# Order of the seven block products in the feed-forward down projection, and the order of token tiles in the last two

## The chip, the cores and the metric

The kernel runs on one core of one Trainium2 chip. The metric is the device time of one execution in microseconds (us). A core has a matrix engine (PE, with its own queue for weight loads, PEld), a vector engine (DVE), a scalar engine (ACT), a general engine (POOL), and a queue engine (SP) that only issues DMA transfers. Each takes its own list of instructions in order; semaphores tie them together. Matmul results go to PSUM, in banks of 128 partitions by 512 float32; everything else is in SBUF.

## The reference

A trunk of two encoder layers on 512 tokens of width 1024. Layer 0 mixes tokens by dilated window attention, layer 1 by latent attention; behind each mixer stands a squared-ReLU MLP of width 4096:

```python
def sq_relu_mlp(h, w1, w2):
    a = jax.nn.relu(h @ w1)
    return (a * a) @ w2

for i in range(DEPTH):
    h = rms_norm(x, norm_mix[i])
    x = x + (dilated_mixer(h, ...) if i % 2 == 0 else mla_mixer(h, ...))
    h = rms_norm(x, norm_ffn[i])
    x = x + sq_relu_mlp(h, ffn_w1[i], ffn_w2[i])
```

The change touches the second product of the MLP, `(a * a) @ w2`, in both layers.

## The kernel before

**Precision.** Every float32 operand of these matmuls is split into a rounded part and a rest: ACT copies the value to `hi` (type fp32r), DVE subtracts to get `lo`. A product of two such values is three matmuls: hi·hi, hi·lo, lo·hi. So each weight tile costs one ACT and one DVE instruction ahead of its matmuls. The split weights (`whi`, `wlo`) sit in four buffers each, in turn; a fifth split waits until the matmuls have let go of the first.

**The MLP** (`mlp`, L592). The width 4096 is cut into four pieces `ch` of 1024. `up(ch, grp)` (L597) makes half a piece: four 128-row groups of `a2`, each by 48 matmuls of 512 columns over four weight units (`run_block`, L161), then Relu and Square on ACT (L615, L616). `down(ch)` (L620) multiplies the piece by its 1024 rows of `w2` and adds it to `resid`. The order is up(0,0), up(0,1), then for each of three pieces up(ch+1,0), down(ch), up(ch+1,1), and at the end down(3). So the last piece stands directly behind up(3,1), which makes the second half of the very piece that it reads; the others have half an up block between.

**The down product** (`wino`, L489). The 512 x 1024 by 1024 x 1024 product is done as a 2 x 2 block product with seven block products in place of eight. `Aq(i, j)` is the block of token half i and inner half j: rows 4j to 4j+3 of `a2` (so `Aq(0, 0)` needs only what up(ch,0) made, and every `Aq(., 1)` needs up(ch,1) too). Three of the left operands are sums of blocks, made on DVE into the two tiles `S["c"]` and `S["d"]` (`stmp`, L514): product 5 uses c = Aq(1,0) - Aq(1,1); product 3 uses d = c - Aq(0,0) and then c = d + Aq(0,1); product 6 uses d; product 7 uses c = Aq(0,0) - Aq(1,0). Products 1, 2 and 4 read blocks of `a2` as they are. Each left operand is split by `split_a` (L483) into one of four `asp` buffers.

The right operands are blocks of `w2` or sums of them, built by DMA in four slots of `wqs`. A plain block is fetched on SP (L511). A sum is a plain fetch and then an accumulating DMA on POOL (L509) onto the same slot; slot `sT` serves 5, then has a block added for 6, then another for 4. The adding DMA has to wait until the earlier product's splits have read the slot. Slots change roles from piece to piece (L583 to L586): the next piece's `sT` is this piece's slot of product 3, its slot of product 1 is this piece's of product 7, of 3 this piece's of 1 (and 2), and of 7 this piece's `sT`.

**Chains and banks.** A product is 24 matmuls: two halves u of the inner dimension, two token tiles t, two 128-rows each, three matmuls. `ORDER` (L588) gives each product a chain of two PSUM banks. Chain a (pool `sc_p`) takes products 1, 6, 7 and 4, each added onto the sum before; chain b takes 5 and 3, chain d product 2, both in pool `tp_p`. After each product `put` (L551) adds the chain's two banks onto a block of `resid` on DVE, one instruction a token tile. A product that adds onto a chain can't write a bank before `put` of the product before it has read it.

**What follows the last piece.** `done` is called for each finished block of `resid`. In layer 1 it writes the block out (L912). In layer 0 (`done0`, L659) it starts the norm of a token tile once both column halves are complete (`norm_tile`, L206: square on ACT, power on POOL, scaling on DVE, then transposes on PE into `tp_p` banks and the split of the result by ACT and DVE into `hT`), and the latent projection of layer 1 (`b_w_in`, L862) follows, 24 matmuls of 448 columns for each of four token tiles.

**Order of execution.** The context at L941 asks for a planned schedule: each engine's list isn't the written order but one that a planner lays out under the written dependencies. In the trace the first half of product 2 runs ahead of product 7, though it is written behind it.

Of the kernel before, what the change touches and what calls it, by code (L numbers as in the profile page):

```python
# [13 lines left out]
ALU = mybir.AluOpType  # L14
# [73 lines left out]
def encoder_kernel(ctx: ExitStack, tc: tile.TileContext, x, norm_mix, norm_ffn, a_w_qkv, a_q_gain, a_k_gain,  # L88
# [6 lines left out]
    def nm(s):  # L95
        uid[0] += 1
        return f"{s}_{uid[0]}"
# [13 lines left out]
    acc_p = ctx.enter_context(tc.tile_pool(name="acc_p", bufs=4, space=PSUM))  # L111
    tp_p = ctx.enter_context(tc.tile_pool(name="tp_p", bufs=2, space=PSUM))
    sc_p = ctx.enter_context(tc.tile_pool(name="sc_p", bufs=2, space=PSUM))
# [369 lines left out]
    def split_a(x, pool):  # L483
        t = pool.tile([P, 4, 2, 256], F32R, tag="asp", name=nm("asp"), bufs=4)
        A.activation(t[:, :, 0], x, AF.Copy)  # L485
        V.tensor_tensor(t[:, :, 1], x, t[:, :, 0].bitcast(F32), op=ALU.subtract)
        return t

    def wino(tag, Aq, w, wqs, pool, resid, done=None):  # L489

        v = w.rearrange("(k p) c -> p k c", p=P)
        S = {}
        slots = SLOTS[tag % 4]  # L500

        def fetch(slot, key, add=False):

            ki, ni = key
            for u in range(2):
                t = wqs[:, 2 * slot + u]
                src = v[:, 4 * ki + 2 * u:4 * ki + 2 * u + 2, 512 * ni:512 * ni + 512]
                if add:
                    nc.gpsimd.dma_start(t, src, accum_op=ALU.add)  # L509
                else:  # L510
                    nc.sync.dma_start(t, src)  # L511
            return [wqs[:, 2 * slot + u] for u in range(2)]

        def stmp(name, x, y, op):  # L514
            if name not in S:
                S[name] = pool.tile([P, 4, 256], F32, tag="S", name=nm("S"), bufs=2)
            V.tensor_tensor(S[name], x, y, op=op)
            return S[name]

        def split_w(x):  # L520
            hi = wp.tile([P, 2, 512], F32R, tag="whi", name=nm("whi"))
            lo = wp.tile([P, 2, 512], F32R, tag="wlo", name=nm("wlo"))
            A.activation(hi, x, AF.Copy)  # L523
            V.tensor_tensor(lo, x, hi.bitcast(F32), op=ALU.subtract)  # L524
            return hi, lo

        sT, s1, s3, s7 = slots
        fetch(sT, (0, 0))
        bT = fetch(sT, (0, 1), add=True)
        b1 = fetch(s1, (0, 0))  # L530
        b3 = fetch(s3, (1, 1))
        fetch(s7, (0, 1))
        b7 = fetch(s7, (1, 1), add=True)

        def operands(p):
            if p == 5:
                return stmp("c", Aq(1, 0), Aq(1, 1), ALU.subtract), bT
            if p == 1:
                return Aq(0, 0), b1
            if p == 3:  # L540
                stmp("d", S["c"], Aq(0, 0), ALU.subtract)
                return stmp("c", S["d"], Aq(0, 1), ALU.add), b3
            if p == 6:
                return S["d"], fetch(sT, (1, 1), add=True)
            if p == 7:
                return stmp("c", Aq(0, 0), Aq(1, 0), ALU.subtract), b7
            if p == 2:
                return Aq(0, 1), fetch(s1, (1, 0))
            return Aq(1, 1), fetch(sT, (1, 0), add=True)

        def put(i, n, op, banks):  # L551
            for t in range(2):
                sl = resid[:, 2 * i + t, 512 * n:512 * n + 512]
                V.tensor_tensor(sl, sl, banks[t], op=op)
                if done is not None and p in (2, 4, 6, 7):
                    done(2 * i + t, n)

        banks = {}
        for p, chain, first, (i, n, op) in ORDER:
            a, wq = operands(p)  # L560
            at = split_a(a, pool)
            if first:
                pl, tg = (sc_p, "sc") if chain == "a" else (tp_p, "tp")
                banks[chain] = [pl.tile([P, 512], F32, tag=tg, name=nm(tg)) for _ in range(2)]
            bk = banks[chain]

            tail = done is not None and p == 4
            parts = {}
            for u, t in ((0, 0), (1, 0), (0, 1), (1, 1)) if tail else ((0, 0), (0, 1), (1, 0), (1, 1)):
                if u not in parts:  # L570
                    parts[u] = split_w(wq[u])
                hi, lo = parts[u]
                for j in range(2):
                    k = 2 * u + j
                    ah = at[:, k, 0, t * P:(t + 1) * P]
                    al = at[:, k, 1, t * P:(t + 1) * P]
                    for i_, (lt, rt) in enumerate(((ah, hi), (ah, lo), (al, hi))):
                        PE.matmul(bk[t], lhsT=lt, rhs=rt[:, j], start=(first and k == 0 and i_ == 0),  # L578
                                  stop=(k == 3 and i_ == 2), skip_group_check=True)
            put(i, n, op, bk)  # L580
# [3 lines left out]
    for _ in range(3):  # L584
        t_, p_, q_, r_ = SLOTS[-1]
        SLOTS.append((q_, r_, p_, t_))  # L586

    ORDER = [(5, "b", True, (1, 1, ALU.add)), (1, "a", True, (0, 0, ALU.add)), (3, "b", False, (0, 1, ALU.add)),  # L588
             (6, "a", False, (0, 1, ALU.subtract)), (7, "a", False, (1, 1, ALU.subtract)),
             (2, "d", True, (0, 0, ALU.add)), (4, "a", False, (1, 0, ALU.add))]  # L590

    def mlp(layer, w1, w2, hT_m, resid, pool, done):  # L592
        a2s = {}
# [26 lines left out]
        def down(ch):  # L620
            a2 = a2s.pop(ch)
            wino(layer * 4 + ch, lambda i, j: a2[:, 4 * j:4 * j + 4, 256 * i:256 * i + 256],
                 w2[1024 * ch:1024 * ch + 1024, :], wqs, pool, resid, done if ch == 3 else None)
# [48 lines left out]
    if True:  # L672
        with tc.tile_pool(name="bpool", bufs=1, reuse_waits="tile") as bp, \
# [203 lines left out]
            pend, tail, nxt, pT, pTs = [], [], None, None, None  # L877
            plan = {2: [(kv_chunk, 0)], 3: [(kv_chunk, 1), (kv_chunk, 2)], 4: [(kv_chunk, 3), (q_chunk, 0)],
                    5: [(q_chunk, 1)], 6: [(q_chunk, 2)], 7: [(q_chunk, 3)]}
            for s_ in range(HB * NT + lag):  # L880
                p, c = divmod(s_, 8)
# [4 lines left out]
                if s_ >= lag:  # L886
                    d, h2, r2, f = pend.pop(0)
# [7 lines left out]
                if p + 1 < HB // 2:  # L895
                    if c == 2:
                        nxt = new_pair(p + 1)
                    if s_ < NT - 1:
                        tail = tail + [q_chunk(cur, s_ + 1)]
                    fresh = [fn(nxt, r) for fn, r in plan.get(c, [])]  # L900
                    if c == 7:
                        tail, fresh = tail + fresh, []
                    for f in tail:
                        f()
                    tail = fresh
# [40 lines left out]
```

## Time and profile before

| | us |
|---|---|
| median of three runs | 1466.03 |
| lowest and highest run | 1465.76, 1466.09 |
| the profiled execution | 1465.81 |
| its span in the profile | 1463.5 |
| PE busy, of the span | 1416.1 |
| DVE busy | 888.2 |
| ACT busy | 727.0 |
| POOL busy | 197.3 |
| the down products of layer 0 (start of the first, end of the last matmul) | 637.39 to 905.77 |
| the down products of layer 1 (the same) | 1191.85 to 1459.47 |

The profiled execution is within 0.3 us of the median; the 2.3 us between its time and its span lie ahead of and behind what the profile covers. Nearly the whole span is PE at work, so what counts is the few places where PE stands idle or runs at a lower clock. "Idle before, releaser" in a row of the timeline is how long the engine had been idle ahead of that instruction and what let it go; "PEclk" is the clock granted to PE as a share of the full one.

### The profile page before, as it was taken

How to read it: one execution, taken by the hardware profiler on the slowest of the kernel's cores; microseconds unless marked ns; L12 is line 12 of the kernel's file. 1: busy time of each engine (PE TensorE's matmuls, PEld its weight loads, DVE VectorE, ACT ScalarE, POOL GpSimd, SP SyncE). 2: the span in 40 equal slices, each digit the busy share in tenths (PEclk: the TensorE clock that was granted, in tenths of full speed). 3: DMA queues.
4: the chain of work that ended last, by engine and by line, in shares of the span. 5: the costliest groups of instructions: out<-in, count | busy, mean ns of one | idle time of the engine just before them, and what ended most of it. 6: DMA issues, size and time to landing. Idle time of an engine off the chain costs nothing.

```text
span 1463.5 us, 19306 instructions
## 1 busy us (share of the span) xinstructions
PE 1416.1 (97%) x7116; PEld 1203.2 (82%) x7116; DVE 888.2 (61%) x1421; ACT 727.0 (50%) x1590; POOL 197.3 (13%) x197
## 2 busy tenths in 40 slices
PE   7999999999999999999999989999999999999988
PEld 6889889889988878888888877776778888888877
DVE  6765565656547654364664758588755265574746
ACT  5544455355335623553635445687633453645543
POOL 1120120111011101010110131232201010010100
PEclk9999999999999999999999999999999999999999
DMA  6315214312532335667494843201014758494843
GB/s 226 105 51 166 62 44 138 95 61 67 160 94 65 96 135 154 207 132 213 118 228 105 218 105 81 67 30 30 30 43 127 219 118 227 103 226 120 202 98 87
DMA packets 134813, 177.52 MB, mean 121 GB/s; under 512 B 8768, under 2 KB 73536, under 8 KB 134720
## 3 DMA queue, kind: packets, MB, share of 16 engines
q1 hardware_dynamic: 117312, 142.74, 30.9%
q0 software_dynamic: 17408, 33.56, 14.1%
q8 instruction: 56, 0.92, 0.3%
q14 instruction: 37, 0.30, 0.1%
HBM read 172.07 MB, written 4.19 MB: 120 GB/s over the span
## 4 chain that ended last, share of the span: by engine, by line
PE 91%; DVE 3%; ACT 3%; issue 2%; DMA 1%; POOL 0%; SPq 0%; DVEq 0%; ACTq 0%; POOLq 0%
PE acc L184 57%; PE sc L578 12%; PE tp L578 9%; PE tp L123 4%; PE acc L857 1%; PE acc L833 1%; PE sc L751 1%; PE sco L444 1%; PE sco L440 1%; PE sc L351 1%; DVE wlo L158 1%; PE sc L833 1%; PE sc L344 0%; PE tp L857 0%; PE sc L340 0%
## 5 line engine op out<-in xcount | busy, mean ns | idle before, releaser
L184 PE MATMUL acc<-whi,hT 128*128 128x512 f32 (+2 forms) x1600 | 487.6, 380 | 7.7 <-DVE t L311 2.6
L158 DVE TENSOR_TENSOR wlo<-raw,whi 128x1024 fp32r<-128x1024 f32 (+3 forms) x170 | 195.8, 1156 | 241.1 <-ACT whi L157 236.3
L184 PEld LDWEIGHTS acc<-whi,hT 128*128 128x128 f32 x1600 | 297.0, 190 | 49.6 <-issue 3.2
L184 PE MATMUL acc<-hT_f,whi 128*128 128x512 f32 (+1 forms) x1152 | 322.7, 366 | 1.7 <-DVE resid L639 1.2
L157 ACT ACTIVATE whi<-raw 128x1024 fp32r<-128x1024 f32 (+3 forms) x170 | 170.3, 1005 | 268.3 <-PE acc L184 170.8
L184 PE MATMUL acc<-wlo,hT 128*128 128x512 f32 (+2 forms) x800 | 300.6, 376 | 0.0
L184 PEld LDWEIGHTS acc<-hT_f,whi 128*128 128x128 f32 x1152 | 208.2, 189 | 37.4 <-DVE resid L639 1.6
L524 DVE TENSOR_TENSOR wlo<-wqs,whi 128x1024 fp32r<-128x1024 f32 x112 | 137.1, 1224 | 123.3 <-ACT whi L523 123.2
L184 PE MATMUL acc<-hT_f,wlo 128*128 128x512 f32 (+1 forms) x576 | 207.7, 365 | 0.0
L523 ACT ACTIVATE whi<-wqs 128x1024 fp32r<-128x1024 f32 x112 | 118.8, 1060 | 170.4 <-PE sc L578 60.9
L184 PEld LDWEIGHTS acc<-wlo,hT 128*128 128x128 f32 x800 | 151.8, 190 | 20.0 <-DVE wlo L158 0.5
L578 PE MATMUL sc<-whi,asp 128*128 128x512 f32 x512 | 164.7, 391 | 0.0
L509 POOL DMA_DIRECT2D wqs<-in_ffn_w_dram x64 | 78.2, 1347 | 541.9 <-DVE wlo L524 283.9
L578 PE MATMUL tp<-whi,asp 128*128 128x512 f32 x384 | 125.1, 394 | 8.9 <-ACT asp L485 8.9
L184 PEld LDWEIGHTS acc<-hT_f,wlo 128*128 128x128 f32 x576 | 108.5, 189 | 17.5
L131 POOL TENSOR_TENSOR qrs<-rs_v,nhalf 128x4 f32<-128x4 f32 x48 | 61.5, 1290 | 408.6 <-DVE rs_v L128 394.1
L578 PEld LDWEIGHTS sc<-whi,asp 128*128 128x128 f32 x512 | 96.7, 189 | 20.1
L578 PE MATMUL sc<-wlo,asp 128*128 128x512 f32 x256 | 100.5, 393 | 0.0
L578 PEld LDWEIGHTS tp<-whi,asp 128*128 128x128 f32 x384 | 73.2, 191 | 25.0 <-ACT asp L485 9.7
L578 PE MATMUL tp<-wlo,asp 128*128 128x512 f32 x192 | 75.9, 395 | 0.0
L136 ACT ACTIVATE junk<-acc 128x128 f32<-128x128 f32 x192 | 53.0, 276 | 18.9 <-PE acc L184 13.9
L578 PEld LDWEIGHTS sc<-wlo,asp 128*128 128x128 f32 x256 | 48.6, 190 | 10.3
(185 smaller groups left out, 1771.0 us busy)
## 6 DMA issues: line engine op xcount, KB each, us to landing
wqs<-in_ffn_w_dram SPq DMA_DIRECT2D x80, 512.0 KB, 4.9
raw<-in_ffn_w_dram SPq DMA_DIRECT2D x64, 512.0 KB, 4.1
wqs<-in_ffn_w_dram POOLq DMA_DIRECT2D x64, 512.0 KB, 7.4
raw<-in_a_w_qkv_dram SPq DMA_DIRECT2D x96, 256.0 KB, 3.3
raw<-in_a_w_qkv_dram SPq DMA_DIRECT2D x64, 192.0 KB, 2.7
raw<-in_a_w_o_dram SPq DMA_DIRECT2D x8, 512.0 KB, 3.9
raw<-in_b_w_o_dram SPq DMA_DIRECT2D x8, 512.0 KB, 3.7
xt<-in_x_dram SPq DMA_DIRECT2D x8, 256.0 KB, 5.7
```

The lines of the kernel that those rows point to most:

```text
L123: PE.transpose(o, i, ident)
L131: G.tensor_tensor(out, v[:, :n], nhalf[:, :n], op=ALU.pow)
L136: A.activation(junk, x, AF.Square, scale=1.0 / math.sqrt(dim), accum_out=out)
L157: A.activation(hi[:, :nk, :n], raw[:, :nk, :n], AF.Copy)
L158: V.tensor_tensor(lo[:, :nk, :n], raw[:, :nk, :n], hi[:, :nk, :n].bitcast(F32), op=ALU.subtract)
L184: PE.matmul(accs[o][:, oc], lhsT=lt, rhs=rt, start=(kt == 0 and p_i == 0 and hv == 0), stop=(kt == total - 1 and p_i == 2), skip_group_che ...
L351: PE.matmul(sc[:, r * P:(r + 1) * P], lhsT=qT[:, r * P:(r + 1) * P], rhs=kT[:, r * P:(r + 1) * P], start=True, stop=True)
L509: nc.gpsimd.dma_start(t, src, accum_op=ALU.add)
L523: A.activation(hi, x, AF.Copy)
L524: V.tensor_tensor(lo, x, hi.bitcast(F32), op=ALU.subtract)
L578: PE.matmul(bk[t], lhsT=lt, rhs=rt[:, j], start=(first and k == 0 and i_ == 0), stop=(k == 3 and i_ == 2), skip_group_check=True)
L833: PE.matmul(sc, lhsT=lt, rhs=rt, start=(i == 0), stop=(i == 4))
```

## The change

Three things are edited. The products run in the order 1, 5, 3, 6, 2, 7, 4 in all eight pieces in place of 5, 1, 3, 6, 7, 2, 4, and slot `s1` is fetched ahead of `sT`. In the last piece of each layer (`done` given) the banks of chain d come from the four of `acc_p`, not from `tp_p`. And in those two pieces product 7, like product 4 before, does all of token tile 0 and then all of token tile 1.

```diff
         sT, s1, s3, s7 = slots
+        b1 = fetch(s1, (0, 0))
         fetch(sT, (0, 0))
         bT = fetch(sT, (0, 1), add=True)
-        b1 = fetch(s1, (0, 0))
         b3 = fetch(s3, (1, 1))
...
             if first:
-                pl, tg = (sc_p, "sc") if chain == "a" else (tp_p, "tp")
+                pl, tg = {"a": (sc_p, "sc"), "b": (tp_p, "tp"), "d": (tp_p, "tp")}[chain]
+                if done is not None and chain == "d":
+                    pl, tg = acc_p, "acc"
                 banks[chain] = [pl.tile([P, 512], F32, tag=tg, name=nm(tg)) for _ in range(2)]
...
-            tail = done is not None and p == 4
+            tail = done is not None and p in (7, 4)
...
-    ORDER = [(5, "b", True, (1, 1, ALU.add)), (1, "a", True, (0, 0, ALU.add)), (3, "b", False, (0, 1, ALU.add)),
-             (6, "a", False, (0, 1, ALU.subtract)), (7, "a", False, (1, 1, ALU.subtract)),
-             (2, "d", True, (0, 0, ALU.add)), (4, "a", False, (1, 0, ALU.add))]
+    ORDER = [(1, "a", True, (0, 0, ALU.add)), (5, "b", True, (1, 1, ALU.add)), (3, "b", False, (0, 1, ALU.add)),
+             (6, "a", False, (0, 1, ALU.subtract)), (2, "d", True, (0, 0, ALU.add)),
+             (7, "a", False, (1, 1, ALU.subtract)), (4, "a", False, (1, 0, ALU.add))]
```

## Prediction

> **What bounds the kernel.** The page first.
>
> ```profile
> PE 1416.1 (97%) x7116; PEld 1203.2 (82%) x7116; DVE 888.2 (61%) x1421; ACT 727.0 (50%) x1590; POOL 197.3 (13%) x197
> PE 91%; DVE 3%; ACT 3%; issue 2%; DMA 1%; POOL 0%; SPq 0%; DVEq 0%; ACTq 0%; POOLq 0%
> ```
>
> PE is busy 97% of the span and 91% of the chain that ended last, and the change takes no matmul away. So it can only win where PE idles or runs at a low clock. The waits of PE, by line, say where:
>
> ```profile
> PE tp L578 <- ACT asp L485: 8.9, 2, 4.4
> PE acc L184 <- ACT hT L220: 1.9, 2, 1.4
> PE tp L123 <- DVE hT L221: 1.9, 1, 1.9
> ```
>
> The down products (L578) wait twice, 4.4 us each. No `put` is in the list. Now an undisturbed piece in the chain of waits:
>
> ```profile
> 637.55 5.44 PE tp L578 x24
> 659.31 2.72 PE tp L578 x12
> 662.03 5.44 PE sc L578 x24
> 667.47 2.72 PE tp L578 x12
> ```
>
> 24 matmuls take 5.44 us, one 0.227, seven products 38.1. Half of product 2 (tp, x12) runs ahead of 7 (sc, x24): the planner had filled the place where 7 waits for the `put` of 6. The six inner pieces have no idle PE, so nothing is to be won there.
>
> The timeline at the start of layer 1's last piece:
>
> ```profile
> 1409.42 1.06 ACT L523 ACTIVATE whi<-wqs 128x1024 fp32r<-128x1024 f32 x1 [4.38 <-PE acc L184]
> 1414.66 0.39 PE L184 MATMUL acc<-hT_f,wlo 128*128 128x512 f32 x1
> 1414.89 1.04 ACT L523 ACTIVATE whi<-wqs 128x1024 fp32r<-128x1024 f32 x1
> 1416.45 0.63 ACT L616 ACTIVATE a<-a 128x512 f32<-128x512 f32 x1
> 1417.11 1.23 DVE L517 TENSOR_TENSOR S<-a 128x1024 f32<-128x1024 f32 x1
> 1418.37 1.06 ACT L485 ACTIVATE asp<-S 128x1024 fp32r<-128x1024 f32 x1 [1.29 <-DVE S L517]
> 1419.33 1.04 ACT L485 ACTIVATE asp<-a 128x1024 fp32r<-128x1024 f32 x1
> 1419.48 0.75 PE L578 MATMUL tp<-whi,asp 128*128 128x512 f32 x1 [4.43 <-ACT asp L485]
> 1419.51 1.22 DVE L486 TENSOR_TENSOR asp<-S,asp 128x1024 fp32r<-128x1024 f32 x1
> ```
>
> The last up matmul ends at 1415.05; its Square ends at 1417.08; then c for product 5 on DVE, its split on ACT, and PE starts 4.43 us late. Product 1's split (asp<-a) stands behind all that though it reads only the first half of `a2`. The clock then falls:
>
> ```profile
> 1419.40:1422.90 3.50, 3.42 (x8) 2.75 (x9) 3.50 (x4) 0.98 (x2) 0.00 (x0) 0.52 0.24 92
> 1423.00:1459.40 36.40, 36.40 (x161) 29.84 (x159) 26.66 (x30) 15.36 (x15) 2.44 (x2) 1.00 0.31 80
> 865.00:870.40 5.40, 5.38 (x13) 4.24 (x14) 4.46 (x4) 1.82 (x2) 5.40 (x6) 0.54 0.15 59
> 1459.51 0.69 DVE L554 TENSOR_TENSOR resid<-resid,sc 128x512 f32<-128x512 f32 x1 [2.03 <-PE sc L578]
> ```
>
> In these windows (length, then busy time and count of PE, PEld, DVE, ACT, POOL, then clock) 8 matmuls take 3.42 us in place of 1.81 in layer 1 and 13 take 5.38 in place of 2.95 in layer 0: 1.6 and 2.4 us lost to a clock of 0.52 to 0.54.
>
> **Part 1: product 1 first.** Counted whole, layer 1's last piece runs from 1415.05 to its last `put` at 1459.51, so PE needs 44.4 for 38.1 us of matmuls: 6.3 us too many. Layer 0's has the same 4.43 and 2.4 for the clock, 6.8. Together **13.1 us**. With 1 first, its left operand depends on up(3,0) alone. Its weights are split in time: the four `whi` buffers let three units of a piece be split before the last up matmul (the third at 1409.42) and the fourth at 1414.89. So 1 starts as the up block ends, and covers 5.44 us, to 1420.49. Product 5 needs its hi part by then (there at 1418.37 + 1.06 = 1419.43 now) and its lo part by its third matmul, at 1420.94 (now 1419.51 + 1.22 = 1420.73). It fits by 0.2 us. But 3's first weight unit comes free half a product on, at 1417.77, and its ACT copy (1.04) may go in front and delay both by 0.5, and in layer 0 POOL works beside these DVE steps:
>
> ```profile
> 862.65 1.22 DVE L517 TENSOR_TENSOR S<-a 128x1024 f32<-128x1024 f32 x1
> 865.19 1.48 DVE L486 TENSOR_TENSOR asp<-S,asp 128x1024 fp32r<-128x1024 f32 x1
> 865.55 1.44 POOL L689 TENSOR_TENSOR cgB<-ck,gr 128x128 f32<-128x128 f32 x1
> ```
>
> There the step takes 0.26 longer. Behind it DVE owes c and d for 3, its lo part, two `put`s and two weight rests by product 3's start, some 7 steps of 1.22 in the 8.8 us from 1417.11 to 1425.93: a stall of 0 to 1.5. I take 0.8 a piece: 13.1 - 1.6 = 11.5: **-11.5 us**.
>
> [...]
>
> **Part 2: the neighbours on one chain.** Before, 6 and 7 stood together on chain a. Now 5 and 3 do (chain b), and 7 and 4 (chain a).
>
> ```profile
> 642.54 1.28 DVE L554 TENSOR_TENSOR resid<-resid,tp 128x512 f32<-128x512 f32 x2
> ```
>
> Product 5 ends at 642.99 by the chain; its first `put` (half of 1.28) ends at 643.18, and 3 must wait for that, 0.2 us, with a signal's delay some 0.5 if nothing fills. From below 0: 6 and 7 met the same and cost nothing, filled by 2. Here product 6's first half can fill after 5, and the next up block after 7 (L184 did so beside product 4). In the two last pieces 7 goes tile by tile, so that pair has half a product, 2.72 us, of cover. That leaves 14 places, 0 to 0.5 each: 0 to 7. By the nearest row, a filled place, the price is near 0; I take 0.15 each, **+2.0 us**.
>
> **Part 3: fetches.** The two adds for 6 wait for 5's splits, now units 3 and 4 of the piece:
>
> ```profile
> 633.01 1.23 DVE L524 TENSOR_TENSOR wlo<-wqs,whi 128x1024 fp32r<-128x1024 f32 x1 [3.30 <-ACT whi L523]
> 638.47 1.22 DVE L524 TENSOR_TENSOR wlo<-wqs,whi 128x1024 fp32r<-128x1024 f32 x1 [4.23 <-ACT whi L523]
> 660.44 1.23 DVE L524 TENSOR_TENSOR wlo<-wqs,whi 128x1024 fp32r<-128x1024 f32 x1 [0.30 <-ACT whi L523]
> 630.02 1.20 POOL L509 DMA_DIRECT2D wqs<-in_ffn_w_dram  x1 [3.34 <-DVE wlo L524]
> 650.19 3.68 POOL L509 DMA_DIRECT2D wqs<-in_ffn_w_dram  x3 [2.40 <-DMA wqs<-in_ffn_w_dram]
> wqs<-in_ffn_w_dram SPq DMA_DIRECT2D x80, 512.0 KB, 4.9
> wqs<-in_ffn_w_dram POOLq DMA_DIRECT2D x64, 512.0 KB, 7.4
> ```
>
> The second moves from 630.02 to about 639.7 and lands 7.4 later, 647.1 (with the issue's 1.2 added, 648.3). Product 6's second half is used at 653.87 + 2.72 and split 2.3 before: 654.3. Cover 6 us, price 0. Behind these adds POOL has only other adds. The fetch for 2 keeps its distance to 1; slot `s1` of the next piece is freed by 7, later than before, but two half up blocks of 96 matmuls, 43 us (one, 21.8, before the last piece), follow.
>
> **Part 4: the border of layer 0.** Rows 0 and 1 are normed once 2 is in `resid`:
>
> ```profile
> 905.38 0.39 PE L578 MATMUL sc<-whi,asp 128*128 128x512 f32 x1
> 900.57 1.28 DVE L554 TENSOR_TENSOR resid<-resid,tp 128x512 f32<-128x512 f32 x2
> 907.45 1.07 ACT L220 ACTIVATE hT<-tp 128x512 fp32r<-128x512 f32 x2
> 908.08 0.47 PE L184 MATMUL acc<-whi,hT 128*128 128x448 f32 x1 [1.44 <-ACT hT L220]
> 908.87 1.09 DVE L158 TENSOR_TENSOR wlo<-raw,whi 128x896 fp32r<-128x896 f32 x1
> 910.61 0.60 PE L123 MATMUL tp<-ck,xn 128*128 128x128 f32 x3 [1.85 <-DVE hT L221]
> 911.00:914.50 3.50, 3.50 (x12) 3.15 (x11) 2.85 (x5) 1.32 (x2) 0.55 (x1) 0.52 0.63 188
> ```
>
> Product 4 ends at 905.77; then PE idles 1.44 and 1.85 and runs 3.5 us at 0.52, losing 1.75: 5.0 in all. After the change 2 is done two products before the end, at 894.9; its `put` is 5.7 us earlier, and with chain d in `acc_p` the `tp_p` banks are free for the transposes. So `hT` of row 0 is there by 908.5 - 5.7 = 902.8, before PE wants it. What is late next is the fourth weight unit (908.87 + 1.09 = 909.96), whose buffer only 4's last matmul frees; a row takes 24 matmuls of 0.2 (x12 in 3.5 at half clock), so a planner that finishes row 0 first wants it at 905.77 + 3.6 and waits 0.6 to 0.8. Bounds 0 and 5.0; **-4.2 us**.
>
> **Part 5: the rest, 0.** Product 7's tile order frees its first weights 1.36 later, under product 4. Layer 1 still ends with 4, its `put` (0.69) and the output.
>
> Sum: -11.5 + 2.0 - 4.2 = -13.7. The profiled 1465.81 becomes 1452.1; its distance to the median, 0.2 us, is nothing here. **1452.1 us.**
>
> **Rivals.** (a) The start doesn't move far: if the planner takes `a2` as one whole, 1 waits for the last Square too and saves only the DVE step, 1.23 a piece. Against it: rows of `hT` are read at 908.08 while others aren't written. An idle of 3.2 is left, and the clock falls as after 1.44 and 1.85 at 908. Gain 2.5 + 4.2 - 2.0 = 4.7: 1461.1. [...] (b) The border gives nothing, because ACT's list, where row 0's copy stood behind weight copies, stays as it is: 1456.3. (c) No place of part 2 is filled, 14 x 0.5 = 7: 1457.1. (d) The planner starts with 5 as before, or 5's DVE work is only late elsewhere: 1466. (e) **Slower.** The next piece's slot `s1` is now asked for first on SP and is freed by 7. If SP keeps that order, the plain fetch of the next `sT` stands behind it until 7's splits, then in the place of the row at 660.44 and 1.2 long, and 4.9 more, and lands at 666.5; if POOL's list still has the adds onto `sT` ahead of those for 4 (as at 650.19, where 4's two follow one of the next piece's), 4's land at 666.5 + 3.6 + 7.4 = 677.5, and are needed at 670.2 - 2.3: 9.6 us late in each of six pieces, 58 us: 1510. It decides from 2.3 us a piece. Against it: the three adds from 650.19 on took 3.68, so 4's were free to go by about 651.4, and the planner puts ahead what is ready.
>
> **Chances.** The forecast (1447 to 1455) 0.58; (b) 0.12; (c) 0.08; (a) 0.08; (d) 0.07; (e) 0.07. What this kernel's runs can tell from no change is about 0.2%, 2.9 us. Faster 0.86 (forecast, a, b, c), same 0.07 (d), slower 0.07 (e). The range takes in the forecast with nothing lost (13.1 + 5.0: 1447.7, and a little for a planner's luck) and a, b and c: 1446 to 1462; 0.14 is left out.
>
> **What would show it.** Right: PE's wait for asp at L485 is gone from the list, the clock is 1.00 through both last pieces, which take 38 to 39.5 us; the waits for `hT` behind 905 are gone. Wrong: PE waits for `put` (L554) inside the inner pieces, a wait for asp as long as before (a), or weight splits that wait for DMA before product 4 (e).

## The result, and the profile after

The changed kernel takes **1451.68 us** (median of four runs, 1451.33 to 1452.76), the kernel before beside it 1465.89 (four runs): a ratio of 0.9904, 95% interval 0.9887 to 0.9922, so 14.2 us less. The forecast was 1452.1. The total was right; several of its terms were not, and they cancelled. The profiled execution took 1451.78 with a span of 1449.6, 13.9 under the span of before.

The matmul line L578 is L580 in the changed kernel. First the page of after, its busy times and the chain that ended last, then PE's waits (engine, line and what was waited for; us in total, times, longest):

```profile
PE 1410.4 (97%) x7116; PEld 1196.8 (83%) x7116; DVE 887.1 (61%) x1421; ACT 727.2 (50%) x1590; POOL 198.4 (14%) x197
PE 89%; ACT 4%; DVE 3%; DMA 2%; issue 1%; POOL 1%; SPq 0%; DVEq 0%; ACTq 0%; POOLq 0%
```

```profile
PE tp L123 <- DVE xn L212: 9.9, 2, 8.9
PE tp L580 <- DVE asp L486: 2.6, 2, 1.5
PE sc L580 <- ACT asp L485: 0.8, 2, 0.4
```

The 8.9 stands at the start of the kernel, as 8.6 did before; the other 1.0 of that line is new. The same 7116 matmuls are busy 5.7 us less, about what the three stretches at half clock had cost before (1.6, 2.4 and 1.75 in the prediction). The waits for asp fell from 8.9 to 3.4 in all, and what is waited for is another thing: the two 4.4 were for the rounded part of product 5's left operand (ACT, L485), the 1.5 is for the rest of it (DVE, L486). The waits for `hT` behind 905 are gone.

To see where the 13.9 us come from, I cut both executions at rows of PE's timeline: the first down matmul, the end of the last up block of each layer, the end of product 4, the end of the `b_w_in` matmuls. "Inner" is from the first down matmul to the end of the last up block, "piece" from there to the end of product 4, "b_in" from there to the end of the `b_w_in` matmuls, "between" from there to the first down matmul of layer 1. The 168 matmuls of a piece need 38.08 us at 0.2267 each.

| us | before | after | difference |
|---|---|---|---|
| up to the first down matmul | 637.39 | 637.01 | -0.4 |
| inner, layer 0 | 223.20 | 223.21 | 0.0 |
| last piece, layer 0 | 45.18 | 43.18 | -2.0 |
| b_in | 28.66 | 22.52 | -6.1 |
| between | 257.42 | 256.32 | -1.1 |
| inner, layer 1 | 223.20 | 223.20 | 0.0 |
| last piece, layer 1 | 44.42 | 40.13 | -4.3 |

Layer 0's last piece now holds some of the norm: eight transposes with a wait of 1.0 ahead of them (for xn, the scaled row), and two of the `b_w_in` matmuls. The rows are PE's timeline of after:

```profile
894.99 0.39 PE L580 MATMUL sc<-whi,asp 128*128 128x512 f32 x1
896.39 1.09 PE L123 MATMUL tp<-ck,xn 128*128 128x128 f32 x8 [1.01 <-DVE xn L212]
897.24 0.47 PE L580 MATMUL sc<-whi,asp 128*128 128x512 f32 x1
...
900.09 0.36 PE L184 MATMUL acc<-whi,hT 128*128 128x448 f32 x1
900.28 0.37 PE L184 MATMUL acc<-wlo,hT 128*128 128x448 f32 x1
...
908.35 0.47 PE L184 MATMUL acc<-wlo,hT 128*128 128x448 f32 x1 [0.23 <-DVE wlo L158]
```

From 894.99 to 897.24 there would be 0.23 without them, so 2.0 were put in; with 0.4 for the two matmuls, 2.4. Taken out of the piece and put to the border, the start of layer 0's last piece went from 7.1 us over its 38.08 to 2.7 (-4.4), layer 1's from 6.3 to 2.0 (-4.3), and the border gave 6.1 - 2.4 = 3.7.

Now the start of layer 1's last piece, in the timeline of after:

```profile
1405.05 0.39 PE L184 MATMUL acc<-hT_f,wlo 128*128 128x512 f32 x1
1405.28 0.39 PE L580 MATMUL sc<-whi,asp 128*128 128x512 f32 x1
1407.51 1.23 DVE L517 TENSOR_TENSOR S<-a 128x1024 f32<-128x1024 f32 x1
1408.20 1.06 ACT L523 ACTIVATE whi<-wqs 128x1024 fp32r<-128x1024 f32 x1 [0.72 <-PE sc L580]
1408.77 1.22 DVE L517 TENSOR_TENSOR S<-S,a 128x1024 f32<-128x1024 f32 x1
1409.17 1.05 ACT L485 ACTIVATE asp<-S 128x1024 fp32r<-128x1024 f32 x1
1409.92 1.22 DVE L524 TENSOR_TENSOR wlo<-wqs,whi 128x1024 fp32r<-128x1024 f32 x1
1411.05 0.68 DVE L554 TENSOR_TENSOR resid<-resid,sc 128x512 f32<-128x512 f32 x1
1411.65 1.22 DVE L486 TENSOR_TENSOR asp<-S,asp 128x1024 fp32r<-128x1024 f32 x1
1412.92 0.73 PE L580 MATMUL tp<-whi,asp 128*128 128x512 f32 x2 [1.14 <-DVE asp L486]
```

Product 1 starts directly behind the up block, as planned: no idle at 1405.28. The rounded part for product 5 is ready at 1409.17 + 1.05 = 1410.22, so DVE could have begun its rest then. It began at 1411.65: the sum d for product 3 (1408.77), a weight rest (1409.92) and a `put` of product 1 (1411.05) stood in front, and PE waited 1.14. In layer 0 the same wait is 1.50. The clock held, in the windows of after (columns as in the prediction):

```profile
866.50:872.90 6.40, 4.89 (x21) 3.68 (x20) 6.32 (x7) 2.95 (x4) 6.40 (x8) 1.00 0.00 1
1411.80:1419.70 7.90, 6.45 (x27) 5.04 (x28) 7.47 (x9) 4.81 (x6) 1.22 (x1) 1.00 0.22 40
```

An inner piece in the chain of waits of after shows how the neighbours on one chain were filled:

```profile
642.62 5.44 PE tp L580 x24
648.06 2.72 PE sc L580 x12
650.78 5.44 PE tp L580 x24
...
664.38 5.44 PE sc L580 x24
669.82 1.81 PE acc L184 x8
671.63 2.72 PE sc L580 x12
```

Half of product 6 (sc, x12) stands between 5 and 3 (tp, x24), and eight matmuls of the up block between 7 and 4.

### The profile page after: what moved, and what is told of

Same layout as the page of the kernel before. It is cut to its first block, busy times and chain, and to the rows that moved or that the text cites. A ratio compares the mean times of both kernels' runs of the same rounds, so it can differ in the third digit from the quotient of the medians.

```text
span 1449.6 us, 19315 instructions
## 1 busy us (share of the span) xinstructions
PE 1410.4 (97%) x7116; PEld 1196.8 (83%) x7116; DVE 887.1 (61%) x1421; ACT 727.2 (50%) x1590; POOL 198.4 (14%) x197
## 4 chain that ended last, share of the span: by engine, by line
PE 89%; ACT 4%; DVE 3%; DMA 2%; issue 1%; POOL 1%; SPq 0%; DVEq 0%; ACTq 0%; POOLq 0%
PE acc L184 58%; PE sc L580 10%; PE tp L580 7%; PE tp L123 4%; PE acc L859 1%; PE acc L835 1%; PE sc L753 1%; PE sco L444 1%; PE sco L440 1%; PE sc L351 1%; PE sc L835 1%; ACT whi L157 1%; ACT junkb L136 1%; DVE wlo L158 1%; PE tp L859 0%
## 5 line engine op out<-in xcount | busy, mean ns | idle before, releaser
L184 PE MATMUL acc<-hT_f,whi 128*128 128x512 f32 (+1 forms) x1152 | 319.4, 366 | 1.9 <-DVE resid L641 1.2
L580 PE MATMUL sc<-whi,asp 128*128 128x512 f32 x512 | 165.1, 390 | 0.8 <-ACT asp L485 0.8
L580 PE MATMUL tp<-whi,asp 128*128 128x512 f32 x352 | 112.2, 390 | 2.6 <-DVE asp L486 2.6
L580 PEld LDWEIGHTS sc<-whi,asp 128*128 128x128 f32 x512 | 96.1, 188 | 21.6 <-ACT asp L485 1.6
L580 PE MATMUL sc<-wlo,asp 128*128 128x512 f32 x256 | 99.6, 389 | 0.0
L580 PEld LDWEIGHTS tp<-whi,asp 128*128 128x128 f32 x352 | 65.9, 188 | 17.2 <-DVE asp L486 3.5
L580 PE MATMUL tp<-wlo,asp 128*128 128x512 f32 x176 | 68.5, 389 | 0.0
L554 DVE TENSOR_TENSOR resid<-resid,sc 128x512 f32<-128x512 f32 x64 | 43.0, 682 | 24.4 <-PE sc L580 24.4
```

Source lines behind the costliest of these rows:

```text
L184: PE.matmul(accs[o][:, oc], lhsT=lt, rhs=rt, start=(kt == 0 and p_i == 0 and hv == 0), stop=(kt == total - 1 and p_i == 2), skip_group_che ...
```

## The experiments

The theory after the result: product 1 first takes away the long wait at the start of the two last pieces, product 2 ahead of 7 takes away the border, the two add up, and the other edits (banks, tile order) are worth little. What remains at the start is DVE's order. The rivals stand with each run. Every time is beside the kernel before on the same chip; ratios have their 95% interval.

### One part alone: product 1 first, 7 ahead of 2 as before

```diff
-             (6, "a", False, (0, 1, ALU.subtract)), (2, "d", True, (0, 0, ALU.add)),
-             (7, "a", False, (1, 1, ALU.subtract)), (4, "a", False, (1, 0, ALU.add))]
+             (6, "a", False, (0, 1, ALU.subtract)), (7, "a", False, (1, 1, ALU.subtract)),
+             (2, "d", True, (0, 0, ALU.add)), (4, "a", False, (1, 0, ALU.add))]
```

> Order 1, 5, 3, 6, 7, 2, 4: product 1 first as in the changed kernel, but 2 behind 7 as before; the rest as changed. Theory (two separate gains, the start of the last pieces some 8 to 9 us and the border of layer 0 some 4 to 5): the start stays won, the border is lost, 1455.5 to 1457.5 us. Rival 1 (all of it is the start): 1451 to 1453. Rival 2 (all of it is the border and what follows): 1464 to 1466.

Measured: 1462.35 (11 runs, 1460.14 to 1466.56) against 1465.51, ratio 0.9983 (0.9973 to 0.9993). A miss by 5 us. The profiled execution, 1465.52, is 3.2 over the median. In it layer 1's last piece took 41.15, but layer 0's took 46.62. PE's waits of this run, and its timeline on POOL and ACT:

```profile
PE acc L580 <- ACT whi L523: 3.0, 1, 3.0
PE sc L580 <- DVE resid L554: 1.1, 2, 0.7
```

```profile
864.21 1.19 POOL L691 TENSOR_TENSOR cgB<-ck,gr 128x128 f32<-128x128 f32 x1 [5.49 <-DMA gr<-in_b_q_gain_dram]
...
873.20 1.19 POOL L509 DMA_DIRECT2D wqs<-in_ffn_w_dram  x1
879.50 2.01 ACT L523 ACTIVATE whi<-wqs 128x1024 fp32r<-128x1024 f32 x2 [5.92 <-DMA wqs<-in_ffn_w_dram]
```

The 3.0 is a wait for weights, and in layer 0 alone. From 864.21 to 873.20 POOL builds small tables (`cgB`, `sgB`) for layer 1's mixer, and the second add onto `sT` goes behind them. ACT waits 5.92 for what it brings, the splits of later products stand behind that in ACT's list, and PE meets them at product 2, the one in an `acc` bank. The last wait, 1.1 in two (0.7 and 0.4), is 7 behind 6 at the `put`: without 2 between them that pair isn't fully filled. Behind the waits of 3.0 and 0.7 the clock fell as well, to 0.62 from 889.30 to 893.80 (11 matmuls from 889.35 to 893.52 took 4.17 us where 0.2267 each make 2.49). The border is no shorter than before, 29.52 against 28.66.

### The other part alone: 2 ahead of 7, product 5 first as before

```diff
-    ORDER = [(1, "a", True, (0, 0, ALU.add)), (5, "b", True, (1, 1, ALU.add)), (3, "b", False, (0, 1, ALU.add)),
+    ORDER = [(5, "b", True, (1, 1, ALU.add)), (1, "a", True, (0, 0, ALU.add)), (3, "b", False, (0, 1, ALU.add)),
```

> Order 5, 1, 3, 6, 2, 7, 4: 2 ahead of 7 as in the changed kernel, but 5 first as before; the rest as changed. Theory: PE waits 4.4 us twice for asp again and the clock falls to half behind it; only the border is won: 1460 to 1462.5 us. Rival 1 (all is the start): 1465 to 1466. Rival 2 (all is the border): 1451 to 1453.

Measured: 1458.59 (5 runs) against 1465.51, ratio 0.9948 (0.9934 to 0.9961), some 1.4 us better than expected. PE's waits have the old one back:

```profile
PE tp L580 <- ACT asp L485: 8.9, 2, 4.4
```

The pieces are as before (46.32 with the norm's work in it, and 44.43), b_in is 22.43. Last piece and b_in of layer 0 together are 68.75 in place of 73.84: the border alone gives 5.1.

### The order alone

```diff
-                if done is not None and chain == "d":
-                    pl, tg = acc_p, "acc"
...
-            tail = done is not None and p in (7, 4)
+            tail = done is not None and p == 4
```

> The changed order alone: chain d stays in the two tp banks and product 7 of the last pieces goes half by half. Theory (these two edits are worth nothing by themselves): 1451 to 1453 us. Rival (the transposes of rows 0 and 1 need the tp banks free, or 4 waits for the put of 7 without the tile order): up to 4 us of the border and 0.5 us a last piece are lost, 1453.5 to 1457.

Measured: 1452.39 (4 runs) against 1465.51, ratio 0.991 (0.9896 to 0.9923); the changed kernel's 0.9904 lies well inside. The banks of chain d and product 7's tile order are together worth nothing that can be measured.

### Product 2 behind 1, in the two last pieces

If DVE is late for product 5, another product that needs only the first half of `a2` can stand ahead of it:

```diff
-        for p, chain, first, (i, n, op) in ORDER:
+        for p, chain, first, (i, n, op) in (ORDER if done is None else LAST):
...
+    LAST = [(1, "a", True, (0, 0, ALU.add)), (2, "d", True, (0, 0, ALU.add)), (5, "b", True, (1, 1, ALU.add)),
+            (3, "b", False, (0, 1, ALU.add)), (6, "a", False, (0, 1, ALU.subtract)),
+            (7, "a", False, (1, 1, ALU.subtract)), (4, "a", False, (1, 0, ALU.add))]
```

> The changed kernel, but in the two last pieces the order is 1, 2, 5, 3, 6, 7, 4: product 2 needs no sum of blocks, so 5's sum has two products of cover in place of one. Theory (what is left of the start's stall is the DVE list ahead of 5's lo part, 1.5 + 0.4 us in layer 0 and 1.1 + 0.3 in layer 1): the waits for asp at 5 and behind are gone, 1447.5 to 1449.5 us. Rival (the same DVE work only comes due later, at 3, or 2's weights come late from their DMA): 1451 to 1454.

Measured: 1455.68 (5 runs) against 1465.51, ratio 0.9932 (0.992 to 0.9945): slower than the changed kernel, a miss by 6 us. Layer 1's last piece is the shortest so far, 39.64, and no wait for asp is left; layer 0's is 47.56. The wait in it, and POOL's timeline of this run:

```profile
PE sc L580 <- ACT whi L523: 5.6, 1, 5.6
```

```profile
864.66 1.50 POOL L695 TENSOR_TENSOR cgB<-ck,gr 128x128 f32<-128x128 f32 x1 [26.71 <-DMA gr<-in_b_q_gain_dram]
...
875.79 2.50 POOL L509 DMA_DIRECT2D wqs<-in_ffn_w_dram  x2
```

Here both adds for product 6 stand behind the tables, and POOL itself had waited 26.7 us for a small transfer (`gr`) that the tables read. Behind the 5.6 the clock fell too, to 0.50 from 883.30 to 886.80 (seven matmuls from 883.30 to 886.45 took 3.15 us where 0.2267 each make 1.59). So two misses had the same place, and I formed a second theory: POOL's list, with the tables in it, is what costs in layer 0.

### The tables later

The tile `gr` is put into free columns of `gl`. Its transfer and the tables then wait until `gl`'s buffer is free, behind the last piece. Nothing computed changes.

```diff
-            gr = bp.tile([P, 2, RD], F32, name="gr")
+            gr = gl[:, QL + KVL:QL + KVL + 2 * RD].rearrange("p (t d) -> p t d", t=2)
```

On the changed kernel:

> The changed kernel with the rotary gains of layer 1 (gr) loaded into free columns of the gain tile gl, so that the nine table instructions on POOL can only run after the norms of layer 0's last piece, not inside that piece. Theory (in layer 0's last piece the second add for 6 now queues behind these instructions and their DMA on POOL, 872.9 in place of about 862, and DVE steps beside them are longer): the piece takes 41.5 to 42.5 us in place of 43.2, the whole 1450 to 1451. Rival (PE waits for no weight there, so the late add costs nothing; the tables come due later instead): 1451.5 to 1453.

On product 1 first alone:

> Order 1, 5, 3, 6, 7, 2, 4 with the tables late. Theory (with 1 first alone layer 0's last piece lost its gain to the tables on POOL: 46.6 us, with a wait of 3 us for 2's weights, against 41.2 in layer 1): the piece falls to 42 to 43, the whole to 1457 to 1459.5. Rival (the order 7, 2 itself makes the late weights): the piece stays at 46 to 47, the whole at 1461 to 1463.

On product 2 behind 1:

> Order 1, 2, 5, 3, 6, 7, 4 in the last pieces, and the tables late as in e5_tables_late. Theory (that order lost 4 us only because 6's weights came late in layer 0, behind the tables on POOL; in layer 1, where there are none, it gained 0.5): layer 0's last piece falls from 47.6 to 41 to 42.5 us, the whole from 1455.7 to 1449 to 1451. Rival (6's weights are late anyway, since 5's splits come one product later than in the changed kernel): the piece stays over 45, the whole 1453 to 1456.

Measured, against 1466.02 for the kernel before: **1450.15** (median of 5 runs: four from 1448.36 to 1451.72, and one of 2878.69 that no trace explains and that the ratio leaves out), ratio 0.9896 (0.9881 to 0.9912), layer 0's piece 41.46; **1457.66** (5 runs), 0.9946 (0.9934 to 0.9959), piece 41.16; **1449.91** (4 runs), 0.9892 (0.9879 to 0.9906), piece 40.58. All three pieces are down, the two that had missed by 5.5 and 7.0 us. POOL's timeline of the first of them:

```profile
860.82 1.20 POOL L509 DMA_DIRECT2D wqs<-in_ffn_w_dram  x1 [4.25 <-DVE wlo L524]
...
912.74 0.46 POOL L692 TENSOR_TENSOR sgB<-ck,gl 128x128 f32<-128x128 f32 x1
```

The second add goes at 860.82 in place of 872.89 in the changed kernel, and the tables at 912. The second theory holds: the misses were the tables ahead of the adds, and the clock that fell behind those waits. With the tables out of the way the two parts of the change add up: product 1 first alone gives 8.4 (1457.66 against 1466.02), 2 ahead of 7 alone gave 6.9 (1458.59 against 1465.51), both together, with the tables later, give 15.9. What is left in the last pieces with product 2 behind 1 is a `put`, in PE's waits of that run:

```profile
PE tp L580 <- DVE resid L554: 1.8, 2, 0.9
```

Product 3 waits 0.9 us in each last piece for the `put` of 5: the very wait that the prediction priced for neighbours on one chain, here with only two matmuls of product 6 to fill it.

### Is the order in which the steps are written what delays product 5's rest?

In the last pieces the split of product 5's left operand is written ahead of product 1's weights.

```diff
+        nxt = None
+        for pi, (p, chain, first, (i, n, op)) in enumerate(ORDER):
+            if nxt is None:
+                a, wq = operands(p)
+                nxt = split_a(a, pool), wq
+            at, wq = nxt
+            nxt = None
+            if done is not None and pi == 0:
+                a, wn = operands(ORDER[1][0])
+                nxt = split_a(a, pool), wn
```

> The changed kernel, but in the two last pieces the left operand of 5 is written ahead of product 1's weights, matmuls and put, so that the planner ranks its split before the put of 1 and 3's weights. Theory (what is left at the start is the DVE list: 5's lo part stands behind one weight rest and one put of 1): the waits at 5 fall from 1.5 and 1.1 to about 0.5 each, 1450 to 1451 us. Rival (ACT's copy for 3's first weights still goes in front and DVE's work comes due at 3 instead): 1451.3 to 1452.5.

Measured: 1451.29 (4 runs) against 1466.02, ratio 0.9901 (0.9887 to 0.9915). PE's waits are those of the changed kernel:

```profile
PE tp L587 <- DVE asp L486: 2.6, 2, 1.5
```

The written order doesn't set it; that theory fell. What ranks a weight rest and a `put` ahead of product 5's rest in the planner I didn't find out.

### Three kernels once more, side by side

The changed kernel, the tables later, and product 2 behind 1 with the tables later, on one chip:

> The changed kernel unaltered, on the same chip as the next two, to compare them without a change of chip. 1451 to 1452.5 us.

> The kernel of e5_tables_late once more. Theory (the late add and the slower DVE steps cost 1.7 us in layer 0's last piece, and nothing is given back): 1.2 to 2.2 us under e10_changed_again. Rival (the 1.5 us of the first comparison came from another chip): within 0.7 us of it.

> The kernel of e6_one_two_tables_late once more. Theory (order 1, 2, 5 saves another 0.9 us in layer 0's last piece and 0.4 in layer 1's, and the stage between the layers is no longer by itself): 1 to 1.5 us under e11_tables_late_again. Rival (the planner's order between the layers, 1.1 us longer there, takes it back): within 0.7 us of it.

Measured, against 1465.3 (7 runs): 1452.11, 1451.6 and 1450.12 (4 runs each), ratios 0.9911 (0.9897 to 0.9926), 0.9907 (0.9892 to 0.9922) and 0.9895 (0.9878 to 0.9911). The tables later gave 0.5 where 1.2 to 2.2 were expected, product 2 behind 1 another 1.5. The stages are steadier than the times: layer 0's last piece and b_in took 64.75, 63.90 and 63.04, layer 1's last piece 40.16, 40.13 and 39.69. So the tables are worth 0.9 and product 2 behind 1 is worth 1.3 by stage. My 1.7 for the tables came from one execution: the changed kernel's first profile held the 1.01 wait for xn, and its second did not. By stage and median the last kernel is the best of all, 2 us under the changed one; the intervals overlap, so the times alone don't settle it. Between the layers the three took 256.15, 257.57 and 257.55; the tables later had also shown 256.40, product 2 behind 1 only 257.49, so that it loses some there isn't excluded.

### A clock that dips or doesn't

The same code, between the layers, took 257.57 us in the second profiled execution of the kernel with the tables later and 256.40 in the first. A window of the second, then of the first:

```profile
925.00:975.00 50.00, 45.49 (x230) 35.58 (x231) 40.59 (x133) 41.95 (x162) 18.76 (x28) 0.97 0.19 59
```

```profile
925.00:975.00 50.00, 44.69 (x232) 33.73 (x230) 41.20 (x132) 42.31 (x164) 19.81 (x28) 1.00 0.15 47
```

The second has the clock (the number after POOL's) at 0.97, here and from 1075 to 1125; the first has 1.00 in both. In the kernel before, the window shown was at 0.97 and in the changed kernel at 1.00 (both had the later one at 1.00). So the -1.1 between the layers in the table above is not shown to be the change's doing: one kernel run twice differs by as much there. The -0.4 ahead of the first down matmul is no different: the same two executions reach it at 637.48 and 635.17.

## Why the prediction was right, and where it wasn't

| term | forecast | profiled executions |
|---|---|---|
| Part 1, start of both last pieces | -11.5 | -8.7 |
| Part 2, neighbours on one chain | +2.0 | 0.0 |
| Part 3, fetches | 0 | 0 for the weights; some 1.0 by way of xn, counted in part 4 |
| Part 4, border | -4.2 | -3.7 |
| stages that the change doesn't touch | 0 | -1.5 |
| sum | -13.7 | -13.9 |

**Part 1: right mechanism, size off by 2.8.** Product 1 starts as the up block ends, the waits of 4.4 are gone, the clock is 1.00 in both windows at the start. But the stall that stays is 2.7 and 2.0 us a piece, not 0.8, and over the bounds of 0 to 1.5 too. The idle in front of product 5 alone was 1.50 and 1.14, and 0.43 and 0.33 came ahead of product 6. The rest, 0.8 and 0.6, isn't idle time: behind an idle PE is slow to get going (the two matmuls at 1412.92 take 0.73, two in a full stretch 0.62); where all of it goes isn't shown. "It fits by 0.2 us" assumed that product 5's rest starts as soon as its rounded part is there; the step that failed is what goes in front on DVE. I had named the weight rest and the `put` as debts that fall due by product 3; the planner paid them first. ACT's weight copy in front of the rounded part (1408.20) did what was said, some 0.4. That the clock held isn't certain either: in the execution of the order alone it fell at this very place (last section).

**POOL beside DVE in layer 0.** By the row of before a DVE step beside POOL's tables takes 0.26 longer, 1.48 in place of 1.22. In the last piece of after, layer 0's two idles are together 0.46 longer than layer 1's (1.93 against 1.47), and with the tables later they are the same in both layers (1.13 and 0.33). In the five table steps that took 1.43 to 1.44, DVE's step had begun first, by 0.2 to 0.4 (last section). No run here turns the order round.

**Part 2: wrong by its 2.0.** All six inner pieces take 223.20 a layer with their up blocks, before and after; each place was filled as the chain shows, and PE waits for no `put` in the last pieces either. The value "near 0" that the nearest row gave was the right one, and the 0.15 a place on top had no row behind it. Rival (c) falls with it. The price itself is real: 0.4 and 0.7 where 7 stood behind 6 without 2 between, 0.9 where product 3 had too little to fill. The forecast's "some 0.5" a place held 0.3 for a signal's delay, which no run shows: PE starts 0.05 behind the end of the DVE step that it waits for (1411.65 + 1.22 = 1412.87, and 1412.92).

**Part 3: right for the inner pieces, wrong in one sentence.** "Behind these adds POOL has only other adds" doesn't hold in layer 0's last piece. POOL's timeline of after:

```profile
857.21 1.20 POOL L509 DMA_DIRECT2D wqs<-in_ffn_w_dram  x1 [20.56 <-DVE wlo L524]
864.01 1.08 POOL L691 TENSOR_TENSOR cgB<-ck,gr 128x128 f32<-128x128 f32 x1 [5.60 <-DMA gr<-in_b_q_gain_dram]
...
871.50 1.44 POOL L692 TENSOR_TENSOR sgB<-ck,gr 128x128 f32<-128x128 f32 x1
872.89 1.19 POOL L509 DMA_DIRECT2D wqs<-in_ffn_w_dram  x1
```

The prediction quoted one of these tables, at 865.55, for its effect on DVE, and didn't ask what it does to the adds once they move past it. The cover of 6 us was just enough here, so PE didn't wait for weights; in the two orders with product 2 elsewhere it was not, and PE waited 3.0 and 5.6. But the late add wasn't free here either. The chain that ended last runs through the tables and this add, then along ACT's and DVE's lists to the wait for xn at 896.39:

```profile
872.89 6.32 DMA wqs<-in_ffn_w_dram
...
895.05 1.30 DVE xn L212
...
896.39 1.09 PE tp L123 x8
```

In the second execution of the same kernel the tables began 0.45 earlier, the add went at 871.80, and PE didn't wait for xn.

POOL's list taken in order is the mechanism of rival (e), with another thing in front and in one piece of eight. Its own form, SP's order of the next piece's slots, cost nothing: the inner pieces are unchanged.

**Part 4: right, 0.5 short in this execution.** Row 0 is there before PE wants it, no `hT` wait is left, and the fourth weight unit costs 0.23 where 0.6 to 0.8 were allowed. What took some of it was the wait of 1.01 for xn (part 3), which the second execution of the same kernel doesn't show; alone, without product 1 first, the border gave 5.1. The loss of before may itself be partly chance: product 1 first alone had nearly the same two idles there with the tables early and late, once with a fall of the clock and once without (last section), in 29.52 and 26.92.

**Rivals (a), (b) and (d)** fall: product 1 doesn't wait for the last Square, the border did give, and the first products did move. Of what would show it, "38 to 39.5 us" for the last pieces was wrong: 40.13, and 40.8 without the norm's work.

So the forecast came within 0.4 us because 2.8 and 0.5 too much in two terms were made up by 2.0 that didn't come and by 1.5 from stages that the change doesn't touch. The mechanisms of parts 1 and 4 were right; that the total came so close is luck.

## What to carry to other kernels

When a transfer's issue moves, read the whole list of the engine that issues it around the new place, compute of other stages included: a few small tables on POOL cost up to 7 us in one piece (47.56 against 40.58 with product 2 behind 1), the fall of the clock behind the wait included, and nothing in seven others. A chain of steps "in time by 0.2" on an engine that has other work ready can be late by one or two of those steps (here by 1.43 us, 1411.65 against 1410.22); price it with them in front. And check a right total stage by stage before believing its terms.

## What the runs showed of the hardware

**The clock falls after the same idles in one execution and not in another.** At the border with product 1 first and the tables early, in PE's timeline and in the windows:

```profile
911.77 1.12 PE L123 MATMUL tp<-ck,xn 128*128 128x128 f32 x4 [2.20 <-DVE hT L221]
```

```profile
912.00:915.50 3.50, 3.50 (x12) 3.20 (x12) 2.70 (x5) 1.33 (x2) 0.55 (x1) 0.50 0.56 180
```

and with the tables late, the same two views:

```profile
906.29 0.66 PE L123 MATMUL tp<-ck,xn 128*128 128x128 f32 x4 [2.26 <-DVE hT L221]
```

```profile
906.30:910.00 3.70, 3.70 (x22) 3.46 (x23) 3.10 (x5) 1.48 (x3) 0.55 (x1) 1.00 0.72 198
```

Idles of 0.87 and 2.20 were followed by 3.5 us at 0.50, idles of 0.81 and 2.26 by none; the border stages are 2.6 us apart. In another run the fall came behind a single idle. At the start of layer 0's last piece, in PE's timeline of the order alone:

```profile
868.02 0.83 PE L578 MATMUL tp<-whi,asp 128*128 128x512 f32 x2 [1.79 <-DVE asp L486]
869.08 1.48 PE L578 MATMUL tp<-whi,asp 128*128 128x512 f32 x3
```

The clock was 0.57 from 868.00 to 871.50: nine matmuls from 868.02 to 871.63 took 3.61 us where 0.2267 each make 2.04. In the second execution of the changed kernel an idle of 1.74 at the same place was followed by 1.00 from 868.30 to 871.80, 15 matmuls in 3.56 us from 868.36 on where 3.40 would do. The prediction took the fall after 1.44 and 1.85 as a rule; these pairs make it a chance, and how great a one they are too few to show. What differs between the two executions of a pair isn't shown. The waits of 4.4 were followed by the fall in all four cases that the kernel before and the order 5, 1, 3, 6, 2, 7, 4 give: to 0.54 and 0.51 from 865.00 to 870.40 in layer 0; in layer 1 to 0.52 before, and with that order eight matmuls from 1412.96 to 1416.48 took 3.52 us in place of 1.81. The one of 5.6 was followed by it as well, at 0.50.

**Beside each other, POOL's steps lengthened more than DVE's.** Late, with little DVE work beside it, a table step of 128 x 128 takes 0.46 us (912.74 above). In the last piece of after, beside DVE's steps with two inputs in SBUF, five of eight take 1.43 to 1.44 (871.50 above); DVE's own go from 1.22 to between 1.30 and 1.49. Each of the five begins 0.2 to 0.4 after such a DVE step has begun and ends 0.3 after that step's end. The two short ones, 0.45 and 0.46, fall beside a `put`, whose second operand is in PSUM; the first of them:

```profile
866.10 0.67 DVE L554 TENSOR_TENSOR resid<-resid,sc 128x512 f32<-128x512 f32 x1
866.47 0.45 POOL L691 TENSOR_TENSOR cgB<-ck,gr 128x128 f32<-128x128 f32 x1
```
